# PEER's expert weights: one-hot products into a ring on chip in place of indirect DMAs into a table in DRAM

## The chip, the cores and the metric

The kernel runs on one core of a Trainium2 chip. The metric is the time of one execution on the device in microseconds (us), and the program's own span is what the profile shows. TensorE (PE in the rows) multiplies matrices, VectorE (DVE), ScalarE (ACT) and GpSimd (POOL) do the work on elements, SyncE (SP) issues the loads of the weights. SBUF is the memory on chip, PSUM holds what TensorE sums up, DRAM lies off the chip.

## The reference

One block of a recurrent and attention mixture, with a PEER layer at its end, and after it a second block with four feed-forward parts and two attentions; 256 tokens of 1024 channels, all in fp32. The change is in the PEER layer, which picks 16 of 16384 experts for each of eight heads:

```python
q = (xt @ w_q).reshape(BLOCK, PEER_HEADS, PEER_QDIM)
s1 = jnp.einsum('chd,nd->chn', q[..., :half], keys1).astype(jnp.float32)
s2 = jnp.einsum('chd,nd->chn', q[..., half:], keys2).astype(jnp.float32)
t1, i1 = lax.top_k(s1, PEER_TOPK)
t2, i2 = lax.top_k(s2, PEER_TOPK)
cand = (t1[..., :, None] + t2[..., None, :]).reshape(BLOCK, PEER_HEADS, PEER_TOPK * PEER_TOPK)
ts, sel = lax.top_k(cand, PEER_TOPK)
idx = jnp.take_along_axis(cidx, sel, axis=-1)
g = jax.nn.softmax(ts, axis=-1)
act = jax.nn.gelu(jnp.einsum('chkd,cd->chk', u[idx], xt))
coef = (g * act.astype(jnp.float32)).astype(xt.dtype)
return jnp.einsum('chk,chkd->cd', coef, v[idx])
```

An expert's number is 128 times a key of the first half plus a key of the second, so a token's weights g are a table of 128 x 128 with at most 128 cells that are not zero.

## The kernel before, in words

The kernel does not gather experts. It multiplies all 16384 rows of u with all 256 tokens, takes the gelu, multiplies it by the table of weights G, which is zero at experts that were not chosen, and multiplies that by all rows of v. Weights come in chunks of 128 x 1024 in an order that the list `plan` fixes: a DMA on SP's queue (L117) brings a chunk into one of five `raw` places, ScalarE rounds it to float32r (`whi`, L107), VectorE subtracts that from the raw chunk (`wlo`, L125, in `losplits`), and TensorE multiplies three times (hi by hi, hi by lo, lo by hi; L153 to L155 for a column block, L165 to L169 for a row block). `pump` issues these up to three chunks ahead. Every engine works in the order of the program text.

The PEER part (`peer`, L744) has this order. For each of the eight heads, `query` multiplies two chunks of query weights and scores the two halves against the keys (L779); then QB = 7 blocks of u follow (`ublock`, with the gelu at L860, kept for two blocks in one of RING = 49 tiles of `acts`). Between the blocks `topk_step` lets VectorE do some steps of the pending `unit`s: the first number of steps is BURST times PACE a block, later PACE = 1.75. A unit is one head: four top-16 searches of 128 scores and two of 256 sums (L784 to L789, L804), the softmax (L811, L812, L830 to L832), the chosen keys by one-hot products of 16 x 16 (L824 to L827) and the addresses (L835, L837). At its end it issues 32 indirect DMAs on POOL, 16 for each half of the tokens, one weight per partition each, that add to G in DRAM, with a memset of one element (`spacer`, L841) ahead of each:

```python
for j in range(16):
    nc.gpsimd.memset(spacer, 0.0)
    x = nc.gpsimd.indirect_dma_start(
        out=G, out_offset=bass.IndirectOffsetOnAxis(ap=ad[:, tb, j:j + 1], axis=0),
        in_=gg[:, tb, j:j + 1], in_offset=None, compute_op=OP.add)
```

`gg` has three buffers, so a head's softmax waits for the DMAs of an earlier head. G was set to zero during block 1 by 64 stores of 256 KB on SP's queue (`zero_g`, L742). After 98 blocks of u, POOL loads G in pieces of four blocks (`gload`, L899), VectorE multiplies the gelu by it (L912), `coef` splits the result (`chi`, `clo`, L182, L183), and the rows of v follow, 128 chunks, with the last 30 blocks of u one by one between the first 30 rows. Then come the residual with block 1's final norm, and block 2, which uses the same places for weights and two more of hi and lo each.

Of the kernel before, what the change touches and what calls it, by code (L numbers as in the profile page):

```python
# [8 lines left out]
F32 = mybir.dt.float32  # L9
F32R = mybir.dt.float32r  # L10
# [7 lines left out]
KB = 8  # L18
# [9 lines left out]
RING = 49  # L28
PACE = 1.75
QB = 7  # L30
BURST = 1.4
NBURST = 16
GB = 4
# [12 lines left out]
for _n, _w in (("ident", 128), ("ones", 128), ("iota16", 16), ("tok", 2), ("half", 2)):  # L46
    CST[_n] = (_off, _w)
    _off += _w
# [16 lines left out]

class Net:
    def __init__(self, ctx, tc, A):
        self.tc, self.nc, self.A = tc, tc.nc, A
        self.base = ctx.enter_context(tc.tile_pool(name="base", bufs=1))
        self.raws = ctx.enter_context(tc.tile_pool(name="raws", bufs=5))  # L70
        self.his = ctx.enter_context(tc.tile_pool(name="his", bufs=4))
        self.los = ctx.enter_context(tc.tile_pool(name="los", bufs=4))
# [3 lines left out]
        self.RA, self.SA, self.bufs, self.lim = 5, 3, 4, None  # L76
        self.pools = [(self.his, self.los)]
        self.b2 = 1 << 30
        self.side = []
# [3 lines left out]
        self.ones = self.c("ones")  # L83

# [9 lines left out]
    def pump(self, i, ahead=None):  # L94
        """loads, hi parts (ahead of chunk i) and, one chunk behind them, lo parts"""
        nc = self.nc
        ahead = self.SA if ahead is None else ahead
        self.prefetch(i)
        lim = len(self.plan) if self.lim is None else self.lim
        self.losplits(max(i, self.si - 1))  # L100
        while self.si < min(i + ahead + 1, lim, self.di):
            j = self.si
            self.losplits(j - 1)
            hp, lp = self.pools[0 if j < self.b2 or (j - self.b2) % 6 < 4 else 1]
            self.hi[j] = hp.tile([128, 1024], F32R, name="whi")
            self.lo[j] = lp.tile([128, 1024], F32R, name="wlo")
            nc.scalar.activation(self.hi[j], self.raw[j], AF.Copy)  # L107
            self.si += 1
            if j <= i:
                self.losplits(j)  # L110

    def prefetch(self, i):
        nc = self.nc
        while self.di < min(i + self.RA, len(self.plan)):
            j = self.di
            self.raw[j] = self.raws.tile([128, 1024], F32, name="raw")
            nc.sync.dma_start(out=self.raw[j], in_=self.plan[j])  # L117
            self.di += 1
            if self.side and j >= 10:
                self.side.pop(0)()  # L120

    def losplits(self, n):
        while self.li <= n and self.li < self.si:
            j = self.li
            self.nc.vector.tensor_sub(out=self.lo[j], in0=self.raw.pop(j), in1=self.hi[j].bitcast(F32))  # L125
# [8 lines left out]
    def chunks(self, n):  # L134
        """n chunks that are in use together"""
        i = self.ci
        self.pump(i, self.bufs - 1)
# [19 lines left out]
    def row_a(self, acc, w, xT, k, first, last):  # L157
        """acc[tb*2+half][tokens, 512] += x[tokens, row block k] w[row block k, 1024 columns]."""
# [19 lines left out]
    def split(self, hi, lo, src, scale=None):  # L178
        """hi + lo = src (times a per-partition scale)."""
# [8 lines left out]
    def tail(self, acc, rows):  # L188
        """the last row blocks, one accumulator after the other; rows: (w, xT, k)"""
# [10 lines left out]
    def rstd(self, r, a, b, p=128):  # L200
        """r = (a + b + eps) ** -0.5, one column"""
# [50 lines left out]
    def to_T(self, outs, x, dg, by_k=False):  # L252
        """channel-major halves of gain * (x * r); outs: (xT, gain), with all but the first left to be called"""
# [1201 lines left out]
```

## Time and profile before

| | |
|---|---|
| median of three runs | 2266.77 us (2264.26 to 2267.86) |
| span of the profiled execution | 2265.6 us (no other time of it is given) |
| TensorE busy | 2027.9 us, 90% |
| VectorE busy | 1292.5 us, 57% |
| ScalarE busy | 1065.4 us, 47% |
| GpSimd busy | 559.0 us, 25% |
| read from and written to DRAM | 367.58 MB and 17.96 MB |

How to read it: busy times are sums over the whole program, and the stages have different limits, so a share says little by itself. TensorE's busy time counts instructions in flight. A row of a group gives busy time in us and the mean length of one instruction in ns; consecutive instructions of one engine overlap a little, so their sum exceeds the time they fill. "Idle before" names what the engine waited for. PEclk is the clock that TensorE was granted, 1.00 being 2.4 GHz and 0.50 being 1.2 GHz.

### The profile page before, as it was taken

How to read it: one execution, taken by the hardware profiler on the slowest of the kernel's cores; microseconds unless marked ns; L12 is line 12 of the kernel's file. 1: busy time of each engine (PE TensorE's matmuls, PEld its weight loads, DVE VectorE, ACT ScalarE, POOL GpSimd, SP SyncE). 2: the span in 40 equal slices, each digit the busy share in tenths (PEclk: the TensorE clock that was granted, in tenths of full speed). 3: DMA queues.
4: the chain of work that ended last, by engine and by line, in shares of the span. 5: the costliest groups of instructions: out<-in, count | busy, mean ns of one | idle time of the engine just before them, and what ended most of it. 6: DMA issues, size and time to landing. Idle time of an engine off the chain costs nothing.

```text
span 2265.6 us, 35450 instructions
## 1 busy us (share of the span) xinstructions
PE 2027.9 (90%) x13868; PEld 1843.6 (81%) x13868; DVE 1292.5 (57%) x2242; ACT 1065.4 (47%) x1623; POOL 559.0 (25%) x687
## 2 busy tenths in 40 slices
PE   8999999975655029999999999999999999999998
PEld 8977999975655029988888899987999999988998
DVE  6565789855542015556666655559654654576444
ACT  5565565532332014444444544467544544466443
POOL 1211138888888850000000100002000000010000
PEclk9999999997878559999999999999999999999999
DMA  7755857755555236666776555542555455534553
GB/s 243 236 156 152 276 146 178 196 122 103 112 121 113 0 65 212 207 214 232 242 235 236 193 193 187 180 164 97 174 187 195 159 188 193 188 111 141 194 194 113
DMA packets 150455, 387.85 MB, mean 171 GB/s; under 512 B 49408, under 2 KB 51968, under 8 KB 150288
## 3 DMA queue, kind: packets, MB, share of 16 engines
q1 hardware_dynamic: 107520, 366.30, 48.8%
q0 software_dynamic: 41616, 17.58, 6.7%
q8 instruction: 108, 1.77, 0.3%
q10 hardware_dynamic: 1152, 1.71, 0.3%
q14 instruction: 59, 0.48, 0.1%
HBM read 367.58 MB, written 17.96 MB: 170 GB/s over the span
## 4 chain that ended last, share of the span: by engine, by line
PE 59%; POOL 10%; DVE 4%; issue 2%; ACT 1%; DMA 0%; POOLq 0%; DVEq 0%; ACTq 0%
PE b L153 10%; PE b L155 9%; PE b L154 9%; PE acc L165 9%; PE acc L167 9%; POOL coef L842 9%; PE acc L169 9%; DVE wlo L125 2%; PE acc L196 1%; PE acc L198 1%; PE acc L197 1%; PE acc L260 0%; DMA coef<-gg,ad 0%; PE b L1231 0%; PE b L1079 0%
## 5 line engine op out<-in xcount | busy, mean ns | idle before, releaser
L125 DVE TENSOR_TENSOR wlo<-raw,whi 128x1024 fp32r<-128x1024 f32 x660 | 784.6, 1225 | 97.2 <-ACT whi L107 89.7
L107 ACT ACTIVATE whi<-raw 128x1024 fp32r<-128x1024 f32 x660 | 678.0, 1052 | 208.5 <-issue 83.0
L155 PE MATMUL b<-xhi,wlo 128*128 128x256 f32 x2416 | 678.8, 281 | 84.0 <-DVE wlo L125 84.0
L153 PE MATMUL b<-xhi,whi 128*128 128x256 f32 x2416 | 680.3, 282 | 0.4 <-DVE lb L1081 0.4
L154 PE MATMUL b<-xlo,whi 128*128 128x256 f32 x2416 | 677.2, 280 | 0.0
L155 PEld LDWEIGHTS b<-xhi,wlo 128*128 128x128 f32 x2416 | 462.7, 192 | 86.1 <-DVE wlo L125 86.0
L153 PEld LDWEIGHTS b<-xhi,whi 128*128 128x128 f32 x2416 | 457.5, 189 | 5.1 <-DVE lb L1081 0.6
L154 PEld LDWEIGHTS b<-xlo,whi 128*128 128x128 f32 x2416 | 457.1, 189 | 3.8
L842 POOL DMA_INDIRECT coef<-gg,ad x256 | 431.1, 1684 | 93.5 <-issue 92.4
L165 PE MATMUL acc<-whi,chi 128*128 128x512 f32 x500 | 158.0, 397 | 122.8 <-ACT chi L182 122.8
L203 POOL TENSOR_SCALAR r<-ss 128x1 f32<-128x1 f32 x16 | 4.7, 297 | 856.6 <-ACT acc L230 487.9
L165 PEld LDWEIGHTS acc<-whi,chi 128*128 128x128 f32 x500 | 92.1, 189 | 143.3 <-ACT chi L182 123.0
L1002 DVE TENSOR_TENSOR silu<-silu,b 128x256 f32<-128x256 f32 x88 | 37.1, 421 | 294.0 <-PE b L155 287.7
L841 POOL MEMSET spacer<- 1x1 f32 x256 | 160.2, 626 | 0.0
L169 PE MATMUL acc<-whi,clo 128*128 128x512 f32 x500 | 157.9, 397 | 0.0
L167 PE MATMUL acc<-wlo,chi 128*128 128x512 f32 x500 | 157.9, 397 | 0.0
L182 ACT ACTIVATE fhi<-silu 128x256 fp32r<-128x256 f32 x88 | 36.8, 418 | 241.4 <-DVE silu L1002 241.4
L183 DVE TENSOR_TENSOR clo<-act,chi 128x512 fp32r<-128x512 f32 x64 | 44.2, 691 | 155.1 <-ACT chi L182 155.1
L182 ACT ACTIVATE chi<-act 128x512 fp32r<-128x512 f32 x64 | 40.3, 630 | 182.5 <-DVE act L912 122.9
L899 POOL DMA_DIRECT2D gt<-coef x32 | 24.1, 754 | 395.0 <-DVE act L912 393.0
L912 DVE TENSOR_TENSOR act<-act,gt 128x512 f32<-128x512 f32 x64 | 43.9, 686 | 124.0 <-DMA gt<-coef 124.0
L155 PE MATMUL b<-ohi,wlo 128*128 128x256 f32 x400 | 113.2, 283 | 1.5 <-DVE wlo L125 1.5
(384 smaller groups left out, 3307.3 us busy)
## 6 DMA issues: line engine op xcount, KB each, us to landing
raw<-ffn_in SPq DMA_DIRECT2D x176, 512.0 KB
raw<-peer_u SPq DMA_DIRECT2D x128, 512.0 KB
raw<-peer_v SPq DMA_DIRECT2D x128, 512.0 KB
raw<-ffn_out SPq DMA_DIRECT2D x88, 512.0 KB
raw<-w_in SPq DMA_DIRECT2D x38, 512.0 KB
coef<-zeros SPq DMA_DIRECT2D x64, 256.0 KB
gt<-coef POOLq DMA_DIRECT2D x32, 512.0 KB
raw<-peer_wq SPq DMA_DIRECT2D x16, 512.0 KB
```

Source lines behind the costliest of these rows:

```text
L107: nc.scalar.activation(self.hi[j], self.raw[j], AF.Copy)
L125: self.nc.vector.tensor_sub(out=self.lo[j], in0=self.raw.pop(j), in1=self.hi[j].bitcast(F32))
L153: mm(ps, whi[:, s], xhi[:, k, n0:n1], start=(k == 0), stop=False)
L154: mm(ps, whi[:, s], xlo[:, k, n0:n1], start=False, stop=False)
L155: mm(ps, wlo[:, s], xhi[:, k, n0:n1], start=False, stop=(k == nk - 1))
L165: mm(acc[tb * 2 + h], xhi[:, k, t], whi[:, h * 512:(h + 1) * 512], start=first, stop=False)
L167: mm(acc[tb * 2 + h], xhi[:, k, t], wlo[:, h * 512:(h + 1) * 512], start=False, stop=False)
L169: mm(acc[tb * 2 + h], xlo[:, k, t], whi[:, h * 512:(h + 1) * 512], start=False, stop=last)
L182: nc.scalar.activation(hi, src, AF.Copy)
L183: nc.vector.tensor_sub(out=lo, in0=src, in1=hi.bitcast(F32))
L841: nc.gpsimd.memset(spacer, 0.0)
L842: x = nc.gpsimd.indirect_dma_start(out=G, out_offset=bass.IndirectOffsetOnAxis(ap=ad[:, tb, j:j + 1], axis=0), in_=gg[:, tb, j:j + 1], in_ ...
```

## The change

The table of weights is no longer added up in DRAM. The top-k units only note, for each token, head and choice, the two keys and the score (`res`). After the units one softmax over all heads follows, and TensorE transposes the two key tables and the weights so that the 128 pairs of head and choice lie on partitions (`rT`, kept in the second half of h). For one token, `e` is the one-hot matrix of the second keys (128 pairs x 128 keys, made by POOL) and `a` that of the first keys, scaled by the weights (made by VectorE); one fp32 product gives the token's whole 128 x 128 table. Four tokens make a group: their product is multiplied into the gelus that already lie in `ring` (VectorE) and copied to the blocks whose gelu is still to come (ScalarE). `ring` holds the gelus or weights of all 128 blocks, 128 KB in each partition. 64 groups run between 26 blocks of u.

Around this: QB is 6 and PACE 1.7; 66 blocks of u (NU1) are in the head part, two more cover the transposes, 26 are in the loop (NU2 = 28 with those two), 34 between rows of v. The chosen keys' multiplication moves from VectorE to POOL. The weights' places become lists of free slots (`Slots`): two raw places are fixed, three lie in block 1's memory, later in rows of the ring that are not in use, in h (which is saved to DRAM and brought back twelve chunks before the end of v), and in block 2's memory; at most six loads are ahead. Keys are loaded on POOL's queue behind the save of h. The stores of zeros are gone.

```diff
-RING = 49
-PACE = 1.75
-QB = 7
+NU1 = 66
+NU2 = 28
+PACE = 1.7
+QB = 6
...
-        self.RA, self.SA, self.bufs, self.lim = 5, 3, 4, None
+        self.rs, self.hs, self.ls = Slots(), Slots(), Slots()
+        self.places(self.base, 2, 4, 4)
+        self.RA, self.SA, self.done = 6, 3, 0
...
-    def zero_g(self, pool):
...
-            self.side.append(lambda a=a: nc.sync.dma_start(out=gv[a], in_=z))
...
+            ring = one.tile([128, EXP_BLOCKS, S], F32, name="ring")
...
+            nc.gpsimd.dma_start(out=hd_, in_=h_)
+            back = self.b2 - 12
+            self.rs.add(h[:, 0, :], back)
+            for b in (100, 104, 108):
+                self.rs.add(ring[:, b:b + 4, :].rearrange("p a b -> p (a b)"), self.p1 + 16 + NU1)
+            keys = carve((2, 128))
+            nc.gpsimd.dma_start(out=keys[:, 0, :], in_=A["keys1"])
+            nc.gpsimd.dma_start(out=keys[:, 1, :], in_=A["keys2"])
...
                     for j in range(2):
-                        oh = tk.tile([128, 16, 16], F32, name="oh")
...
-                        nc.vector.tensor_mul(out=oh, in0=oh, in1=i12f[:, tb, j, None, :].to_broadcast([128, 16, 16]))
-                        nc.vector.tensor_reduce(out=ex[:, tb, j, :], in_=oh, axis=AX.X, op=OP.add)
...
-                for tb in tbs:
-                    for j in range(16):
-                        nc.gpsimd.memset(spacer, 0.0)
-                        x = nc.gpsimd.indirect_dma_start(
...
+                        nc.gpsimd.tensor_mul(out=oh[:, tb, j], in0=oh[:, tb, j],
+                                             in1=i12f[:, tb, j, None, :].to_broadcast([128, 16, 16]))
+                    late.append(lambda tb=tb: nc.vector.tensor_reduce(out=res[:, 0:2, tb, hk], in_=oh[:, tb], axis=AX.X,
+                                                                      op=OP.add))
...
+                p = self.bank(S)
+                self.lin_b(p, self.chunk(), 0, x2T, KB, 0, S)
+                if n:
+                    nc.scalar.activation(p[:, :n], p[:, :n], AF.Gelu_apprx_tanh)
+                if n < S:
+                    nc.scalar.activation(ring[:, b, n:], p[:, n:], AF.Gelu_apprx_tanh)
+                if n:
+                    nc.vector.tensor_mul(out=ring[:, b, :n], in0=p[:, :n], in1=ring[:, b, :n])
...
-            gload(0)
-            gload(1)
...
+            def onehots(g):
+                if g >= NG:
+                    return
+                t0 = 4 * g
+                e, a = et[g % 3], at[g % 2]
+                for i in range(4):
+                    nc.gpsimd.tensor_scalar(e[:, i, :], iota, rT[:, 1, t0 + i:t0 + i + 1], None, op0=OP.is_equal)
+                for i in range(4):
+                    nc.vector.tensor_scalar(a[:, i, :], iota, rT[:, 0, t0 + i:t0 + i + 1], rT[:, 2, t0 + i:t0 + i + 1],
+                                            op0=OP.is_equal, op1=OP.mult)
+                st[g] = (e, a)
...
+                for i in range(4):
+                    mm(p[:, i * 128:(i + 1) * 128], e[:, i, :], a[:, i, :], start=True, stop=True)
+                pg = p.rearrange("p (t b) -> p b t", b=128)
+                onehots(g + 1)
+                nc.vector.tensor_mul(out=ring[:, :nb, t0:t0 + 4], in0=pg[:, :nb, :], in1=ring[:, :nb, t0:t0 + 4])
+                nc.scalar.activation(ring[:, nb:, t0:t0 + 4], pg[:, nb:, :], AF.Copy)
+                built[0] = g + 1
+
+            onehots(0)
+            g = 0
+            for i in range(2, NU2):
+                ublock(u)
+                u += 1
+                while g * (NU2 - 2) < NG * (i - 1):
+                    group(g, u)
+                    g += 1
...
-                c = act.pop(b2)
-                nc.vector.tensor_mul(out=c, in0=c, in1=gt[b // GB][:, b % GB:b % GB + 2, :].rearrange("p a b -> p (a b)"))
```

On POOL the order before, from the end of block 1 through the PEER part, was this (the two rows that follow each other 256 times stand once):

```order
L203 TENSOR_SCALAR r<-ss 128x1
L204 TENSOR_TENSOR r<-r,cst 128x1
L841 MEMSET spacer 1x1
L842 DMA coef<-gg,ad 4194304x1
...
L842 DMA coef<-gg,ad 4194304x1
L899 DMA gt<-coef 128x4x256 x32
```

and it is now this, from the same place (`work` holds the one-hot matrices, `coef` is the DRAM table, which now only keeps h):

```order
L242 TENSOR_SCALAR r<-ss 128x1
L243 TENSOR_TENSOR r<-r,cst 128x1
L804 DMA coef<-h 128x2048
L810 DMA ring<-keys 128x128
L811 DMA ring<-keys 128x128
L877 TENSOR_TENSOR work<-work,ring 128x256 x32
L968 TENSOR_SCALAR work<-cst,h 128x128 x256
L1020 DMA ring<-final_g 128x512 x2
L1026 DMA h<-coef 128x2048
```

The 256 DMAs and their spacers went, 32 products and 256 one-hots came, and the save of h stands ahead of the keys.

On VectorE, at the end of the last unit and the begin of the v part, the order before was:

```order
L837 SCALAR_TENSOR_TENSOR ad<-ex 128x16
L125 TENSOR_TENSOR wlo<-raw,whi 128x1024 x22
L912 TENSOR_TENSOR act<-act,gt 128x512
L183 TENSOR_TENSOR clo<-act,chi 128x512
L912 TENSOR_TENSOR act<-act,gt 128x512
L183 TENSOR_TENSOR clo<-act,chi 128x512
L125 TENSOR_TENSOR wlo<-raw,whi 128x1024 x4
```

and in the second and third turn of the new loop it is:

```order
L163 TENSOR_TENSOR wlo_70<-raw_61,whi_66 128x1024
L905 TENSOR_TENSOR ring<-b,ring 128x12
L970 TENSOR_SCALAR work<-cst,h 128x128 x4
L983 TENSOR_TENSOR ring<-acc,ring 128x70x4
L970 TENSOR_SCALAR work<-cst,h 128x128 x4
L983 TENSOR_TENSOR ring<-acc,ring 128x70x4
L163 TENSOR_TENSOR wlo_67<-raw_62,whi_63 128x1024
L905 TENSOR_TENSOR ring<-b,ring 128x20
L970 TENSOR_SCALAR work<-cst,h 128x128 x4
L983 TENSOR_TENSOR ring<-acc,ring 128x71x4
```

A turn has one subtraction (L163), the product with the gelu of its own block (L905, waiting for ScalarE), and for each group four one-hots of the next group (L970) ahead of the product into the ring (L983, waiting for TensorE).

## Rows read from the trace of the kernel before

**Rows 1.** Busy time by stretches: PE, PEld, DVE, ACT, POOL, then PEclk, DMA share, GB/s

```profile
299.00:327.40 28.40, 26.95 (x227) 26.13 (x227) 24.98 (x81) 17.26 (x22) 8.16 (x9) 1.00 0.52 156
...
405.60:431.50 25.90, 25.65 (x226) 25.46 (x226) 24.78 (x68) 14.85 (x18) 22.73 (x24) 1.00 0.76 187
550.00:600.00 50.00, 21.00 (x166) 20.80 (x165) 19.76 (x54) 12.76 (x15) 43.38 (x50) 0.69 0.43 73
700.00:750.00 50.00, 11.86 (x105) 11.66 (x103) 4.18 (x4) 5.82 (x7) 43.14 (x54) 0.64 0.37 51
750.00:800.00 50.00, 0.00 (x0) 0.00 (x0) 0.00 (x0) 0.00 (x0) 42.86 (x55) 0.50 0.22 0
```

**Rows 2.** Waits from 280 to 840 us: who waited for whom, total, times, longest

```profile
DVE act L912 <- DMA gt<-coef: 124.0, 1, 124.0
...
DVE gg L811 <- DMA coef<-gg,ad: 94.4, 4, 31.5
...
PE b L155 <- DVE wlo L125: 84.0, 9, 29.0
```

**Rows 3.** Costliest groups, POOL's: busy, mean ns of one, idle time before

```profile
L842 POOL DMA_INDIRECT coef<-gg,ad x256 | 431.1, 1684 | 93.5 <-issue 92.4 <-DVE wlo L125 0.5 <-DVE ex L827 0.3
L841 POOL MEMSET spacer<- 1x1 f32 x256 | 160.2, 626 | 0.0
```

**Rows 4.** ScalarE in order of time, one head: start, us, instruction, idle before

```profile
379.71 0.39 ACT L772 ACTIVATE q<-b 128x256 f32<-128x256 f32 x1 [1.77 <-PE b L155]
...
397.45 0.60 ACT L860 ACTIVATE act<-b 128x512 f32<-128x512 f32 x1 [1.77 <-PE b L155]
402.89 0.60 ACT L860 ACTIVATE act<-b 128x512 f32<-128x512 f32 x1 [1.77 <-PE b L155]
405.62 0.39 ACT L772 ACTIVATE q<-b 128x256 f32<-128x256 f32 x1 [1.17 <-PE b L155]
```

**Rows 5.** TensorE in order of time: PEER's begin and the first row of v

```profile
292.94 1.50 PE L260 MATMUL acc<-dg,h 128*128 128x128 f32 x12
294.20 0.37 PE L153 MATMUL b<-xhi,whi 128*128 128x256 f32 x1
...
834.67 1.22 PE L165 MATMUL acc<-whi,chi 128*128 128x512 f32 x2 [122.81 <-ACT chi L182]
```

**Rows 6.** VectorE's groups by shape: busy, mean ns of one, idle before

```profile
L125 DVE TENSOR_TENSOR wlo<-raw,whi 128x1024 fp32r<-128x1024 f32 x69 | 83.0, 1217 | 9.9 <-ACT whi L107 8.1 <-issue 1.8
L826 DVE TENSOR_TENSOR oh<-oh,i12f 128x256 f32<-128x256 f32 x22 | 9.5, 434 | 0.8
...
L912 DVE TENSOR_TENSOR act<-act,gt 128x512 f32<-128x512 f32 x64 | 43.9, 686 | 124.0 <-DMA gt<-coef 124.0
```

**Rows 7.** VectorE and POOL in order of time, in block 1

```profile
45.85 0.99 DVE L405 TENSOR_SCALAR cd<-cst,cs 128x128 f32<-128x128 f32 x5
46.77 0.40 DVE L483 TENSOR_SCALAR y<-xrp,pv 128x272 f32<-128x272 f32 x1
...
67.91 0.84 POOL L467 TENSOR_TENSOR iy<-iy,y 128x272 f32<-128x272 f32 x1 [2.71 <-ACT iy L466]
68.03 0.88 DVE L483 TENSOR_SCALAR y<-xrp,pv 128x272 f32<-128x272 f32 x1
```

**Rows 8.** POOL's scalings: one line's least, median, most ns; and a group

```profile
L948 POOL TENSOR_SCALAR h<-act,r x4: 683/693/1401, 1284.7 to 1288.0; 128x512 f32<-128x512 f32 x4
...
L203 POOL TENSOR_SCALAR r<-ss 128x1 f32<-128x1 f32 x16 | 4.7, 297 | 856.6 <-ACT acc L230 487.9 <-ACT acc L1325 187.5 <-issue 179.0
```

**Rows 9.** ScalarE in order of time, gelus beside the first rows of v

```profile
848.66 0.60 ACT L860 ACTIVATE act<-b 128x512 f32<-128x512 f32 x1 [1.78 <-PE b L155]
...
859.86 0.60 ACT L860 ACTIVATE act<-b 128x512 f32<-128x512 f32 x1 [1.72 <-PE b L155]
...
871.11 0.60 ACT L860 ACTIVATE act<-b 128x512 f32<-128x512 f32 x1 [1.72 <-PE b L155]
```

**Rows 10.** Busy time in a stretch of block 1, columns as in rows 1

```profile
224.00:232.00 8.00, 6.50 (x52) 6.16 (x52) 6.22 (x10) 7.90 (x16) 4.02 (x4) 1.00 0.07 13
```

More of the change, by code (lines that the diff above doesn't have):

```diff
@@ L63, with __init__, add, take @@
 NC2 = _off
+class Slots:
+    def __init__(self):
+        self.all, self.occ, self.clock = [], {}, 0
+    def add(self, ap, until=1 << 30):
+        self.all.append([ap, until, self.clock])
+    def take(self, j):
+        free = [s for s in self.all if j < s[1] and not any(o is s for o in self.occ.values())]
+        if not free:
+            return None
+        s = min(free, key=lambda s: (s[1], s[2]))
+        self.occ[j] = s
+        return s[0]
+    def free(self, j):
+        self.clock += 1
+        self.occ.pop(j)[2] = self.clock
 class Net:
@@ L83, in __init__, with places @@
         self.ones = self.c("ones")
+    def places(self, pool, nr, nh, nl, until=1 << 30):
+        for n, k, sl in (("raw", nr, self.rs), ("whi", nh, self.hs), ("wlo", nl, self.ls)):
+            for i in range(k):
+                dt = F32 if n == "raw" else F32R
+                sl.add(pool.tile([128, 1024], dt, name=f"{n}{i}", bufs=1), until)
     def c(self, n):
@@ L97, in pump @@
         ahead = self.SA if ahead is None else ahead
+        while self.done < min(i, self.ci):
+            self.hs.free(self.done)
+            self.ls.free(self.done)
+            self.done += 1
         self.prefetch(i)
-        lim = len(self.plan) if self.lim is None else self.lim
         self.losplits(max(i, self.si - 1))
-        while self.si < min(i + ahead + 1, lim, self.di):
+        while self.si < min(i + ahead + 1, self.di):
             j = self.si
             self.losplits(j - 1)
[L104 to L107, printed above, removed]
+            t = self.hs.take(j)
+            if t is None:
+                assert j > i
+                break
+            self.hi[j] = t
+            nc.scalar.activation(t, self.raw[j], AF.Copy)
             self.si += 1
@@ L115, in prefetch @@
             j = self.di
-            self.raw[j] = self.raws.tile([128, 1024], F32, name="raw")
-            nc.sync.dma_start(out=self.raw[j], in_=self.plan[j])
+            t = self.rs.take(j)
+            if t is None:
+                break
+            self.raw[j] = t
+            nc.sync.dma_start(out=t, in_=self.plan[j])
             self.di += 1
-            if self.side and j >= 10:
-                self.side.pop(0)()
     def losplits(self, n):
@@ L300, in block1 @@
             sm = ctx.enter_context(tc.tile_pool(name="b1sm", bufs=2))
+            self.places(one, 3, 0, 0, self.p1)
             def T8(name, dt=F32, n=T):
@@ new lines, in peer @@
+            for c0, n in ((0, 2), (2, 1)):
+                p = self.ps.tile([128, 512], F32, name="acc", tag="acc")
+                for i in range(2 * n):
+                    nc.tensor.transpose(p[:, i * 128:(i + 1) * 128], res[:, c0 + i // 2, i % 2, :], self.ident)
+                nc.scalar.activation(rT[:, c0:c0 + n, :].rearrange("p a b -> p (a b)"), p[:, :n * S], AF.Copy)
+            used[1] = 0
+            et = [carve((4, 128), F32, 1) for _ in range(3)]
+            at = [carve((4, 128), F32, 1) for _ in range(2)]
@@ L935, in peer @@
             self.tail(acc, rows)
-            hg = [acts.tile([128, 512], F32, name="act") for _ in range(4)]
+            hg = [room(20 + 2 * i, 2) for i in range(4)]
             dg, r = self.residual(spool, h, acc, 1.0, (hg, gain), ahead=True)
```

219 lines of the change are left out of this document (110 added, 109 removed).

## The prediction

> **What bounds the kernel now.** I read the busy time by stretches first, then the waits of the PEER part, then the group of POOL's indirect DMAs, then single instructions for their pace. The stretches show where TensorE stops: in the head loop it is busy for 25.65 of 25.90 us, in three later stretches of 50 us for 21.00, 11.86 and 0 us, while POOL is busy for 43 of 50 in all three [rows 1]. The waits name the cause: once, for 124.0 us, VectorE waits for the load of the table of coefficients, and four times, 94.4 us together, it waits at a head's softmax (L811) for an indirect DMA. Behind that wait on VectorE's queue stand the subtractions that make wlo, so TensorE waits 84.0 us for wlo [rows 2]. POOL is the source: 256 indirect DMAs of 1.684 us and as many spacers of 0.626 us, 591 us of POOL's own time [rows 3], where the stretch on TensorE's path takes 834.67 - 294.20 = 540.5 us from the first query matmul to the first row of v [rows 5].
>
> What TensorE itself needs there follows from its pace. Two u blocks take 402.89 - 397.45 = 5.44 us, 2.72 us for one chunk; a head of nine chunks takes 405.62 - 379.71 = 25.91 us, so 1.43 us are left for its four key products [rows 4]. 114 chunks and 8 heads are 321.5 us: 219 us of the 540.5 are waiting.
>
> **The change, part by part.** All POOL work of the stretch, the 124.0 us and the 94.4 us go. In their place, on TensorE's path from 294.20 on:
>
> 1. Sixteen query chunks and 66 u blocks, 82 x 2.72 = 223.0 us, and 8 x 1.43 = 11.4 us of key products.
>
> 2. Stalls of that part. VectorE must keep up. Before, a head had 24.78 us of it [rows 1]; nine subtractions of 1.217 us [rows 6] are 11.0, so 13.8 us are top-k, 15.75 of a unit's 21 steps: 18.4 us a unit. Now four multiplications of 0.434 us [rows 6] go to POOL and the addresses go, some 2.3 us; 16.1 us a unit, of which 13.6 of 17 steps fall on a head, 12.9 us, with eight subtractions 22.6 us against TensorE's 8 x 2.72 + 1.43 = 23.2 us. The cover is 0.6 us a head: thin. I take 5.5 us: 1.45 us as the first head loses now (26.95 busy of 28.40 [rows 1]), the rest for POOL's products and for the keys, which now follow the 1 MB save of h on POOL's queue. The ends are 0 and 22 (32 products of 0.84 us on POOL [rows 7] that all hold VectorE up, less 8 x 0.6).
>
> 3. Two u blocks, 5.4 us, and six transposes at 0.21 us (twelve passes of fp32 128x128 fill 292.94 to 294.20, two to a product [rows 5]), 1.3 us. Scores, softmax and the first one-hot group lie beside these and block 68.
>
> 4. The loop: 26 u blocks with 64 groups of four tokens, 2.46 groups to a block. TensorE: 2.72 + 2.46 x 4 x 0.21 + 0.2 for the changes of type = 5.0 us a turn. VectorE: four one-hots of 128 columns. Five with one scalar of the partition, the last of them shorter, take 0.99 us; with two scalars 272 columns take 0.40 us [rows 7]; I take 0.25 us, 1.0 a group. Then the product of PSUM and ring, 4 x 69 to 94 elements, on average 328: between 0.434 us for 256 and 0.686 us for 512 [rows 6], less some 0.07 us of overlap, 0.43 us. That it steps through the ring in pieces of four no row shows; the pace of whole rows is taken. With one subtraction of 1.2 and 0.3 us for the gelu part: 2.46 x 1.43 + 1.5 = 5.0 us a turn, level with TensorE. POOL: 9.85 one-hots a turn. Between 0.297 us for one column and 0.683 us for 512 [rows 8] a line gives 0.39 us, 3.84 us a turn.
>
> These three don't run freely side by side. A VectorE instruction of 0.40 us took 0.88 us where a POOL product of 0.84 us ran beside it: 0.88 began at 68.03 and ended 0.16 us after POOL did [rows 7]. So a POOL instruction costs VectorE about (0.88 - 0.40)/0.84 = 0.57 of its length, where VectorE reads two operands of SBUF or scales one. Such work is 2.46 x 1.0 + 1.2 = 3.66 of its 5.0 us, 73%. 3.84 x 0.73 x 0.57 = 1.6 us: 6.6 us a turn, 26 x 6.6 = 172 us. The ends: 5.1 us (133 us) without collisions, 8.85 us (230 us) if VectorE's 3.66, POOL's 3.84 and the free 1.35 us come one after the other. I stay at the middle, where the one measured pair lies.
>
> The Trainium skill (SBUF — State Buffer, Who interferes with whom) states it more harshly: VectorE and GpSimd share a pair of ports under an exclusive lock, whoever comes first holds it for the whole instruction, and the other one fully blocks. It speaks against this change; the pair above agrees in kind, but its 0.48 us is less than POOL's 0.84.
>
> 5. The first coefficients wait for the last group's product and their split: 1.5 us, two steps of about 0.69 us [rows 6].
>
> 6. The v part gets four more u blocks beside it, 10.9 us. It runs on TensorE (two rows and two blocks in 871.11 - 859.86 = 11.25 us). Its first pair now takes 848.66 - 834.67 = 14.0 us [rows 5, 9], after 120 us of pause; with the pause those 2.7 us go. The 64 multiplications by the table on VectorE were beside TensorE and give nothing.
>
> 7. At nothing: the 64 stores of zeros (beside block 1's matmuls), h saved and brought back (1 MB each; the load starts eleven rows of v before its use, some 30 us), the new places of the weights (only three raw places in the loop, but a turn there is twice as long as a chunk). If that cover is gone, h back late costs up to 6 us and block 2's first chunks up to 3 us.
>
> Sum: 223.0 + 11.4 + 5.5 + 6.7 + 172 + 1.5 = 420.1 us for 540.5; 120.4 us gained, less 10.9, plus 2.7: 112 us. The profiled execution spans 2265.6 us, and no other time of it is given; the median of the three runs is 1.2 us above. 2265.6 - 112.2 + 1.2 = 2154.6: **2155 us**.
>
> **The rivals.** *No collisions*: POOL runs three groups ahead and meets VectorE only in its PSUM products. The loop is 133 us, the time 2155 - 39 = 2116. For it: POOL has the shorter list; against it: the pair in [rows 7].
>
> *One after the other*: the loop takes 8.85 us a turn, 230 us, and the time is 2213. For it: in [rows 7] neither engine gets on while the other is at it, and 9.85 hand-overs a turn can each cost something; against it: part of VectorE's wait was hidden in its own start. This is the Trainium skill's lock, from the section named above, taken by its word.
>
> *TensorE's clock*: it is granted 0.69 in a stretch where it is busy for 21.00 of 50 us [rows 1], and 1.00 in one where it is busy for 6.50 of 8 [rows 10]. If the loop, busy at 5.0 of 6.6, fell to the lower level of 1.2 GHz, a turn would be 10 us on TensorE, 260 us, the time 2243. Against it: its gaps there are about 1 us each, those of [rows 1] some 30 us.
>
> *Slower than before*: POOL's one-hots become the bound. The gain of 112 us is gone at 284 us for the loop, 10.9 us a turn, 1.11 us for each of the 9.85 one-hots. The longest POOL instruction of this form took 1.401 us, with 512 columns and VectorE beside it [rows 8]; 1.2 us for 128 columns would give 307 us and 2290. For it: no row shows a comparison on POOL. Against it: the same form without VectorE takes 0.683 us for four times the columns.
>
> **How the numbers follow.** My forecast (a turn of 5.7 to 7.3 us) has 0.52, no collisions 0.24, one after the other 0.14, the clock 0.06, slower 0.03, and 0.01 for a loss that just eats the gain. The range takes in the first three: from 2116 less the 5.5 us of stalls, 2110, to 2213. A measurement of this kernel tells some 0.2%, 4.5 us, from no change. Faster 0.96, the same 0.01, slower 0.03.
>
> **What would show it.** Right: no wait for a DMA of coefficients is left; the head loop keeps 2.72 us a chunk; the first row of v starts at about 714 us; in the loop VectorE is the busiest, its four one-hots with POOL beside them take about 1.5 us instead of 1.0, and TensorE waits there for VectorE's one-hots. Wrong: PEclk below 1.0 in the loop (the clock), one-hots on POOL far from 0.39 us, products into the ring far from 0.43 us (the stride), TensorE waiting for POOL rather than VectorE, or wlo late in the head loop (the cover of 0.6 us).

## The result, and the profile after

The changed kernel takes 2177.99 us, median of four runs (2174.22 to 2178.89), against 2265.7 us (2264.26 to 2267.86) of the kernel before: a ratio of 0.961, interval 0.9596 to 0.9623. The forecast was 2155 us with a range of 2110 to 2213. The time lies in the range, 23 us above the forecast. The profiled execution took 2177.61 us, its span is 2175.8 us, 89.8 us shorter than before, where 112.2 were forecast.

The busy time by stretches of the kernel after answers to [rows 1] and shows the loop, 550 to 700 us:

```profile
405.60:431.50 25.90, 25.65 (x220) 25.46 (x219) 21.77 (x62) 12.15 (x15) 3.73 (x4) 1.00 0.52 164
550.00:600.00 50.00, 45.75 (x318) 40.62 (x318) 38.12 (x105) 17.66 (x39) 50.00 (x75) 0.97 0.27 83
600.00:650.00 50.00, 45.05 (x328) 40.29 (x327) 38.36 (x108) 16.97 (x41) 50.00 (x75) 1.00 0.27 85
```

The third number of busy time is VectorE's, the fifth POOL's. In the loop POOL is busy for 50.00 of 50 us and VectorE for 38. VectorE was forecast to be the busiest. The waits from 290 to 730 us, which answer to [rows 2]:

```profile
PEld acc L980 <- POOL work L968: 30.8, 73, 0.7
POOL work L968 <- ACT h L955: 23.1, 1, 23.1
...
PE acc L980 <- DVE work L970: 12.0, 27, 0.6
```

PEld is TensorE's loading of weights. No wait for a DMA of coefficients is left. The products of one-hots (L980) wait first of all for POOL's one-hots (L968), 73 times, and only 27 times for VectorE's (L970). What the two lines take, from the views of the two lines (least, median and most ns, first and last start):

```profile
L968 POOL TENSOR_SCALAR work<-cst,h x256: 596/602/1662, 548.8 to 723.6; 128x128 f32<-128x128 f32 x128
```

```profile
L970 DVE TENSOR_SCALAR work<-cst,h x256: 328/338/481, 549.0 to 723.6; 128x128 f32<-128x128 f32 x128
```

POOL's one-hot takes 0.602 us and not 0.39. The 256 of them fill 175.4 us without a gap (the group's busy time), 0.685 us from start to start on average, and that is the loop.

The average hides two kinds, and the 1662 in the row of L968 points at the second. In each of the 26 turns one of POOL's one-hots runs beside VectorE's subtraction of two tensors, which makes wlo:

```profile
604.33 1.21 DVE L163 TENSOR_TENSOR wlo<-raw,whi 128x1024 fp32r<-128x1024 f32 x1
```

```profile
604.48 1.53 POOL L968 TENSOR_SCALAR work<-cst,h 128x128 f32<-128x128 f32 x1
```

By the timelines of the two engines, all 26 of these take 1.33 to 1.66 us and end 0.40 to 0.48 us after the subtraction; the next one-hot starts 1.52 us after such a one, and 0.59 us after any other. So about 26 x (1.52 - 0.59) = 24 of the 175.4 us are POOL held up by VectorE's subtraction. The subtraction itself keeps its 1.21 us. An estimate from these two figures: without the hold the 256 one-hots would fill 256 x 0.59 = 151 us. What the loop meets then is seen below, in e12_pair.

Where the 89.8 us come from follows from the beginnings of the stages; TensorE's and ScalarE's single instructions of the kernel after (in this order block 1's residual sum, the first PEER matmul, the first row of v, PEER's residual sum, and the first silu, block 2's first activation):

```profile
287.50 0.60 ACT L269 ACTIVATE acc<-h 128x512 f32<-128x512 f32 x1 [1.89 <-DVE h L266]
...
297.57 0.37 PE L192 MATMUL b<-xhi,whi 128*128 128x256 f32 x1
...
726.17 1.22 PE L204 MATMUL acc<-whi,chi 128*128 128x512 f32 x2 [1.48 <-ACT chi L221]
...
1176.17 0.60 ACT L269 ACTIVATE acc<-h 128x512 f32<-128x512 f32 x1 [1.89 <-DVE h L266]
...
1200.59 0.38 ACT L1100 ACTIVATE silu<-b 128x256 f32<-128x256 f32 x1
```

and those of the kernel before, beside [rows 5]:

```profile
284.18 0.60 ACT L230 ACTIVATE acc<-h 128x512 f32<-128x512 f32 x1 [1.89 <-DVE h L227]
...
1275.15 0.60 ACT L230 ACTIVATE acc<-h 128x512 f32<-128x512 f32 x1 [1.89 <-DVE h L227]
...
1292.93 0.38 ACT L1001 ACTIVATE silu<-b 128x256 f32<-128x256 f32 x1
```

| stage | before | after | forecast |
|---|---|---|---|
| to block 1's residual sum | 284.18 | 287.50 (+3.3) | no change |
| first PEER matmul to POOL's first one-hot (548.8) | | 251.2 | 246.6 |
| from there to the first row of v | | 177.4 | 173.5 |
| both together | 540.5 | 428.6 (-111.9) | 420.1 |
| first row of v to PEER's residual sum | 440.5 | 450.0 (+9.5) | +8.2 |
| block 2, from there to the end | 990.5 | 999.6 (+9.2) | no change |

### The profile page after: what moved, and what is told of

Same layout as the page of the kernel before. It is cut to its first block, busy times and chain, and to the rows that moved or that the text cites. A ratio compares the mean times of both kernels' runs of the same rounds, so it can differ in the third digit from the quotient of the medians.

```text
span 2175.8 us, 36723 instructions
## 1 busy us (share of the span) xinstructions
PE 2122.0 (98%) x14386; PEld 1914.6 (88%) x14386; DVE 1349.3 (62%) x2458; ACT 1078.1 (50%) x1720; POOL 309.7 (14%) x436
## 3 DMA queue, kind: packets, MB, share of 16 engines
q8 instruction: 114, 1.87, 0.3%
## 4 chain that ended last, share of the span: by engine, by line
PE 82%; POOL 9%; DVE 5%; issue 2%; ACT 2%; DMA 0%; SPq 0%; POOLq 0%; DVEq 0%; ACTq 0%
PE b L192 15%; PE b L194 15%; PE b L193 15%; PE acc L204 10%; PE acc L206 10%; PE acc L208 10%; POOL work L968 8%; DVE wlo L163 2%; PE acc L235 1%; PE acc L237 1%; PE acc L236 1%; PE acc L299 1%; PE acc L676 0%; PE acc L677 0%; PE b L505 0%
## 5 line engine op out<-in xcount | busy, mean ns | idle before, releaser
L163 DVE TENSOR_TENSOR wlo<-raw,whi 128x1024 fp32r<-128x1024 f32 x451 | 537.4, 1227 | 44.9 <-ACT whi L138 43.2
L138 ACT ACTIVATE whi<-raw 128x1024 fp32r<-128x1024 f32 x451 | 463.8, 1052 | 73.0 <-PE acc L208 43.6
L968 POOL TENSOR_SCALAR work<-cst,h 128x128 f32<-128x128 f32 x256 | 175.4, 706 | 23.1 <-ACT h L955 23.1
L138 ACT ACTIVATE whi<-ring 128x1024 fp32r<-128x1024 f32 x106 | 112.0, 1058 | 114.6 <-issue 43.3
L163 DVE TENSOR_TENSOR wlo<-ring,whi 128x1024 fp32r<-128x1024 f32 x106 | 132.0, 1246 | 12.9 <-ACT whi L138 12.8
L163 DVE TENSOR_TENSOR wlo<-h,whi 128x1024 fp32r<-128x1024 f32 x103 | 126.9, 1232 | 7.6 <-ACT whi L138 7.6
L222 DVE TENSOR_TENSOR clo<-ring,chi 128x512 fp32r<-128x512 f32 x64 | 44.2, 693 | 120.8 <-ACT chi L221 118.9
L206 PEld LDWEIGHTS acc<-wlo,chi 128*128 128x128 f32 x500 | 94.3, 189 | 22.8
L208 PEld LDWEIGHTS acc<-whi,clo 128*128 128x128 f32 x500 | 94.2, 188 | 22.8
L192 PE MATMUL b<-ohi,whi 128*128 128x256 f32 x400 | 112.4, 281 | 0.0
```

The costliest lines, as they stand in the source:

```text
L138: nc.scalar.activation(t, self.raw[j], AF.Copy)
L163: self.nc.vector.tensor_sub(out=t, in0=self.raw.pop(j), in1=self.hi[j].bitcast(F32))
L192: mm(ps, whi[:, s], xhi[:, k, n0:n1], start=(k == 0), stop=False)
L206: mm(acc[tb * 2 + h], xhi[:, k, t], wlo[:, h * 512:(h + 1) * 512], start=False, stop=False)
L208: mm(acc[tb * 2 + h], xlo[:, k, t], whi[:, h * 512:(h + 1) * 512], start=False, stop=last)
L222: nc.vector.tensor_sub(out=lo, in0=src, in1=hi.bitcast(F32))
```

## The experiments

All start from the changed kernel unless they name another. Each ratio is to the kernel before, run on the same chip, with its 95% interval; differences in us to the change are of medians from different chips, so the ratios decide. Two theories stand from the first reading. A: POOL's one-hot simply costs 0.60 us, about 0.69 from start to start, and POOL sets the loop. B: it costs 0.39 us, as forecast, and the rest is waiting for VectorE. C, that TensorE sets the loop, goes along.

**e3_alone.** VectorE's one-hots are left out from the third group on.

```diff
-                for i in range(4):
+                for i in range(4 if g < 2 else 0):
                     nc.vector.tensor_scalar(a[:, i, :], iota, rT[:, 0, t0 + i:t0 + i + 1], rT[:, 2, t0 + i:t0 + i + 1],
                                             op0=OP.is_equal, op1=OP.mult)
```

> Leaves out VectorE's one-hots of expert halves times gate from the third group of four tokens on (the coefficients are wrong after that), so POOL's 256 one-hots run beside a VectorE that has 1.2 us less to do in each of the 64 groups. Theory A (a POOL one-hot costs 0.60 us by itself and about 0.69 from start to start, whatever VectorE does): POOL stays full in the loop, L968 keeps its median of 602 ns, the loop stays at 170 to 178 us and the time within 5 us of 2178. Theory B (it costs about 0.39 us and the rest is waiting for VectorE's accesses): L968 falls to 400 to 500 ns, the loop to what TensorE needs, 26 u blocks x 2.8 + 64 products x 1.05 = 140 us, and the time to about 2145. Theory C (TensorE sets the loop): the time stays, but POOL shows idle time in the loop.

Ratio 0.9593 (0.9574 to 0.9612), 2172.65 us: no difference from the change that can be told. The stretch and POOL's line:

```profile
600.00:650.00 50.00, 47.32 (x332) 40.54 (x331) 20.61 (x35) 17.66 (x42) 50.00 (x74) 1.00 0.25 84
```

```profile
L968 POOL TENSOR_SCALAR work<-cst,h x256: 596/603/1672, 547.8 to 720.7; 128x128 f32<-128x128 f32 x128
```

VectorE falls from 38 to 21 of 50 us, POOL stays at 50 and its one-hot at 0.603 us. A stands for the 0.60 us and for POOL setting the loop, and B falls; C falls too, since POOL has no gap. The step from 0.60 to 0.685 is not A's, though: the subtractions stay in this run, and 26 one-hots of 1.49 to 1.67 us are still there.

**e2_split.** One of POOL's four goes to VectorE.

```diff
-                    nc.gpsimd.tensor_scalar(e[:, i, :], iota, rT[:, 1, t0 + i:t0 + i + 1], None, op0=OP.is_equal)
+                    eng = nc.vector if i == 3 else nc.gpsimd
+                    eng.tensor_scalar(e[:, i, :], iota, rT[:, 1, t0 + i:t0 + i + 1], None, op0=OP.is_equal)
```

> One of POOL's four one-hots in each group goes to VectorE. Theory A: POOL needs 3 x 0.69 = 2.07 us a group in place of 2.76, VectorE 2.2 + 0.3 = 2.5 and becomes the bound, 64 x 2.5 = 160 in place of 177: 15 to 20 us faster, about 2160. Theory B (the two engines exclude each other): what the two need together falls by only 0.1 us a group, 6 us or less: 2172 to 2178. Theory C: no change.

Ratio 0.9567 (0.9551 to 0.9583), 2166.89 us, 11 us less than the change: more than B's 6 and less than A's 15. POOL now stands idle for 44.9 us, waiting for TensorE to free one of the three buffers, and yet TensorE waits 38.2 us for POOL's one-hots and 13.0 for VectorE's. From POOL's first one-hot to the first row of v it is 169.1 us in place of 177.4, 8 us less and not 17; e12_pair shows why.

**e1_wide.** Two POOL instructions of 512 columns in place of four of 128.

```diff
-                for i in range(4):
-                    nc.gpsimd.tensor_scalar(e[:, i, :], iota, rT[:, 1, t0 + i:t0 + i + 1], None, op0=OP.is_equal)
+                nc.gpsimd.tensor_sub(out=e, in0=iota[:, None, :].to_broadcast([128, 4, 128]),
+                                     in1=rT[:, 1, t0:t0 + 4, None].to_broadcast([128, 4, 128]))
+                nc.gpsimd.tensor_scalar(e, e, 0.0, None, op0=OP.is_equal)
```

> POOL makes the four one-hots of a group with two instructions of 128x512 (number minus index for four tokens, then equal to zero) instead of four of 128x128. Theory A with a price that is mostly for the instruction: 1.2 to 1.4 for the subtraction and 0.7 for the comparison, about 2.0 us a group; TensorE (140 us for the loop) and VectorE (2.2 us a group) become the bound: 20 to 30 us faster, about 2153. Theory A with a price that goes by elements: 4 x 0.6 + 4 x 0.7 = 5.2 us a group, 64 x 2.4 more: about 2330. Theory B: more accesses to wait for, slower, 2190 or more. Theory C: no change.

Ratio 0.9701 (0.9679 to 0.9724), 2197.73 us, 20 us slower than the change. Neither price of A was right: the comparison of 512 columns takes 1.49 us, so a column costs (1.490 - 0.602)/384 = 2.3 ns and the instruction itself some 0.3. POOL needs 2.57 us for a group that nothing holds up; with 21 instructions of 2.13 to 2.44 us beside VectorE's subtraction it is busy for (75.6 + 107.8)/64 = 2.87 us a group, where the change has 4 x 0.685 = 2.74. And a new wait appears, in POOL's and VectorE's instructions one by one:

```profile
601.27 1.03 POOL L967 TENSOR_TENSOR work<-cst,h 128x512 f32<-128x512 f32 x1
602.39 1.49 POOL L969 TENSOR_SCALAR work<-work 128x512 f32<-128x512 f32 x1
```

```profile
601.31 1.07 DVE L971 TENSOR_SCALAR work<-cst,h 128x128 f32<-128x128 f32 x1
602.30 0.77 DVE L971 TENSOR_SCALAR work<-cst,h 128x128 f32<-128x128 f32 x1
603.00 0.33 DVE L971 TENSOR_SCALAR work<-cst,h 128x128 f32<-128x128 f32 x1
```

VectorE's one-hot, begun 0.04 us after POOL's subtraction, lasts 1.07 us and ends with it; free of it, it takes 0.33.

**e4_nu2.** Six more blocks of u by the end of the loop.

```diff
-NU2 = 28
+NU2 = 34
```

> 34 blocks of u in place of 28 are computed by the end of the loop (NU2 = 34), so six leave the part of the rows of v. Theory A (and B): POOL paces the loop, 64 x 2.76 = 177 us, in which TensorE has 6 x 2.8 = 17 us to spare; the loop stays at 177 to 182 and the v part shortens by 6 x 2.8: 12 to 17 us faster, about 2163. Theory C: the loop grows by what the v part loses, no change within 4 us.

Ratio 0.9549 (0.9528 to 0.9571), 2162.92 us, 15 us less than the change. The six blocks of u fit under POOL's time: its one-hots run from 549.1 to 730.5, 181.3 us in place of 175.4, and the v part lost 18 us. C falls here too.

```profile
L968 POOL TENSOR_SCALAR work<-cst,h x256: 594/602/1664, 549.1 to 729.9; 128x128 f32<-128x128 f32 x128
```

The 256 one-hots are the same, and so is their median; but six more blocks bring six more subtractions, and by the timeline 32 one-hots in place of 26 are held up. At 0.93 us each that is 5.6 of the 6.0 us by which POOL's time grew.

**e8_price.** What does the 0.60 us pay for? POOL multiplies in place of comparing.

```diff
-                    nc.gpsimd.tensor_scalar(e[:, i, :], iota, rT[:, 1, t0 + i:t0 + i + 1], None, op0=OP.is_equal)
+                    nc.gpsimd.tensor_scalar(e[:, i, :], iota, rT[:, 1, t0 + i:t0 + i + 1], None, op0=OP.mult)
```

> POOL's 256 comparisons become 256 multiplications by the same scalars, of the same size (the coefficients are wrong after that). Theory A1 (the price goes with the operation: on POOL a comparison takes 0.30 us and 2.3 ns a column, which the 0.60 us of 128 columns and the 1.49 us of 512 give, a multiplication 0.30 us and 0.75 ns a column): L968 falls to about 0.39 us, POOL needs under 2 us a group and idles, the loop goes to what VectorE and TensorE leave, 150 to 168 us, and the time to 2150 to 2168. Theory A2 (the price is that of the form, whatever the operation): L968 stays at 0.60, the time at 2174 to 2180.

Ratio 0.9608 (0.9592 to 0.9624), 2176.5 us; A2. The multiplication costs the same:

```profile
L968 POOL TENSOR_SCALAR work<-cst,h x256: 593/599/1662, 548.7 to 723.8; 128x128 f32<-128x128 f32 x128
```

**e9_twoop.** The row that had given 0.39, POOL's scaling of 512 columns in 0.683 us [rows 8], has two operations. So the comparison gets a second one, times 1.0.

```diff
-                    nc.gpsimd.tensor_scalar(e[:, i, :], iota, rT[:, 1, t0 + i:t0 + i + 1], None, op0=OP.is_equal)
+                    nc.gpsimd.tensor_scalar(e[:, i, :], iota, rT[:, 1, t0 + i:t0 + i + 1], 1.0, op0=OP.is_equal,
+                                            op1=OP.mult)
```

> POOL's comparison gets a second operation, times 1.0, as the scalings of POOL in the residual have (0.683 us for 128x512 with two operations, against 1.49 us for 128x512 with one in the run with two wide instructions). Theory F (on POOL the form with one operation is the slow one, whatever the operation): L968 falls to about 0.39 us, POOL needs under 2 us of a group and idles, the loop goes from 177 to 150 to 168 us, and the time to 2150 to 2168. Rival G (the 0.60 us has another cause: the second operand, or the tiles' place): L968 stays at 0.60 or grows, the time at 2174 or more.

Ratio 0.9723 (0.9707 to 0.9739), 2202.11 us. F falls: the second operation costs 0.11 us more.

```profile
L968 POOL TENSOR_SCALAR work<-cst,h x256: 707/713/1772, 547.1 to 748.7; 128x128 f32<-128x128 f32 x128
```

**e12_pair.** What is left of that row is its pair of multiplications.

```diff
-                    nc.gpsimd.tensor_scalar(e[:, i, :], iota, rT[:, 1, t0 + i:t0 + i + 1], None, op0=OP.is_equal)
+                    nc.gpsimd.tensor_scalar(e[:, i, :], iota, rT[:, 1, t0 + i:t0 + i + 1], 1.0, op0=OP.mult,
+                                            op1=OP.mult)
```

> POOL's 256 comparisons become a pair of multiplications, by the same scalar and by 1.0, the form of the scalings in the residual (128x512 in 0.683 us), at 128 columns (the coefficients are wrong after that). Theory H (POOL has a quick path for this pair of operations, and the estimate of 0.39 us was right for it and wrong for a comparison): L968 at 0.35 to 0.45 us, POOL idles in the loop, 2150 to 2168. Rival I (the pair costs what comparison and multiplication cost, 0.71 us; the scalings in the residual are quick for a reason of their own): L968 at 0.65 to 0.75 us and the time near 2200.

Ratio 0.9547 (0.9528 to 0.9566), 2162.56 us. H stands:

```profile
L968 POOL TENSOR_SCALAR work<-cst,h x256: 368/375/1412, 547.8 to 702.6; 128x128 f32<-128x128 f32 x128
```

```profile
600.00:650.00 50.00, 45.74 (x350) 42.82 (x349) 42.81 (x116) 18.02 (x44) 29.56 (x80) 1.00 0.28 85
```

This run is the loop as it was forecast, with one-hots of 0.375 us on POOL. It takes 162 us from POOL's first one-hot to the last product, POOL idles, and the first row of v starts 711.13 - 296.51 = 414.6 us after the first PEER matmul (forecast: 420.1). It also shows the next bound: between two blocks of u two or three groups follow one another, and in such a run each takes 1.29 to 1.41 us (in the middle of the loop 2 groups in 2.58 us, 3 in 4.22), where its eight passes alone take 1.05. TensorE waits there, 19.4 us for POOL's one-hots and 8.8 for VectorE's, while POOL waits 57.2 us for a free buffer: the one-hots are only one or two groups ahead when such a run begins. More buffers, for which no memory is left, were not tried.

**e6_act34.** A way around POOL's price that keeps the computation, on top of e4_nu2: one of four comparisons on ScalarE.

```diff
-                for i in range(4):
+                for i in range(3):
                     nc.gpsimd.tensor_scalar(e[:, i, :], iota, rT[:, 1, t0 + i:t0 + i + 1], None, op0=OP.is_equal)
+                nc.scalar.activation(e[:, 3, :], iota, AF.Square, bias=rT[:, 1, t0 + 3:t0 + 4], scale=-1.0)
+                nc.scalar.activation(e[:, 3, :], e[:, 3, :], AF.Relu, bias=self.ones[:, 0:1], scale=-1.0)
```

> One of POOL's four comparisons goes to ScalarE, as the square of the difference and then 1 minus it, cut at zero; and 34 blocks of u in place of 28 by the end of the loop. Theory A: POOL needs 3 x 0.69 x 64 = 132 us, TensorE 32 x 2.8 + 64 x 1.05 = 157, VectorE about 155; the loop takes 157 to 168 in place of the 182 with 34 blocks alone, 2140 to 2150. Rival (ScalarE, which has the gelus, the copies of the ring's rest and the hi parts before it, delivers the one-hot late): the loop stays over 175 and the time at 2157 or more.

Ratio 0.954 (0.9524 to 0.9556), 2160.47 us: in the rival's range, and not to be told from e4_nu2 by the times. The loop is 175 us (546.9 to 722) where 157 to 168 were expected; ScalarE's two pieces take 0.39 and 0.40 us and the trace shows no wait for them, so the rival's time came and its cause did not. From 550 to 710 us TensorE waits 19.6 us for POOL's one-hots and 13.5 for VectorE's, as in e12_pair in the runs of groups, and POOL 48.6 us for a buffer.

**e5_raws and e10_raws2.** Block 2's first chunks wait for a place. Both kernels give the base pool a third raw place. e5_raws takes its memory by moving the third buffer of POOL's one-hots into the ring's last blocks; e10_raws2 does without that buffer.

```diff
-        self.places(self.base, 2, 4, 4)
+        self.places(self.base, 3, 4, 4)
...
-            et = [carve((4, 128), F32, 1) for _ in range(3)]
+            et = [carve((4, 128), F32, 1) for _ in range(2)]
```

These two edits stand in both kernels, and so does a smaller `work`; e5_raws also has `et.append(sct[0]...)`, the third buffer in its new place, and e10_raws2 takes the two buffers in turn.

> A third place for raw weights in the base pool (its 4 KB come from the third buffer of POOL's one-hots, which moves into memory of the scores, idle by then). Theory P (block 2 starts late because only two of its chunks have a place before the last readers of the blocks of gelu are done): a third chunk of block 2 lies loaded at the residual sum, ScalarE's waits for raw<-ffn_in shrink by about 2.5 to 5 us, the first silu comes 18 to 21 us after the residual sum in place of 24.4, and the time falls by 3 to 6 us to about 2173. Rival (the chunks are late for another reason: POOL's scalings or ScalarE's order): the first silu stays 24 us behind and the time within 1.5 us.

> The third place for raw weights again, now with two buffers of POOL's one-hots in place of three, and none in the ring. The loop is paced by POOL and should grow by 0 to 8 us from the missing buffer. Theory P (block 2 waits for a place): the first silu 20 to 22 us behind the residual sum in place of 24.4. If the loop holds at 177, the time falls by 3 to 5 us.

e5_raws: ratio 0.9706 (0.969 to 0.9722), 2197.43 us. The choice of memory was a mistake of mine: ScalarE copies each group's product into all blocks to the ring's end, so it writes over that buffer (the coefficients are wrong after that), and copy and one-hots wait for each other (ScalarE 34.0 us for POOL); POOL's one-hots now end at 744. The start of block 2 still got shorter, 21.6 us from residual sum to silu.

e10_raws2: ratio 0.9597 (0.9581 to 0.9613), 2174.1 us, too near the change for the times to tell. The trace tells: 1197.06 - 1175.59 = 21.5 us to the first silu in place of 24.4, and ScalarE's waits for the loads went from the first of these rows (change) to the second (e10_raws2):

```profile
ACT whi L138 <- DMA raw<-ffn_in: 4.9, 2, 2.5
```

```profile
ACT whi L138 <- DMA raw<-ffn_in: 2.1, 1, 2.1
```

P stands, for about 3 of the 6.6 us that block 2's start lost: the ten kernels with two places take 23.0 to 25.2 us here, the three with a third place 20.9 to 21.6. Places for more chunks were not tried. The loop did not miss the buffer (548.3 to 722.9).

**e7_block1.** Block 1 prepares 3 chunks ahead where several are taken at once.

```diff
-        self.pump(i, 5)
+        self.pump(i, 3 if i < self.p1 else 5)
```

> In block 1 a call for several chunks prepares 3 chunks ahead, as before the change, and not 5, so that VectorE has one wlo in place of two ahead of the last softmax scaling. Theory S (that second wlo makes TensorE wait 1.9 us for the scaling, after which its clock falls to the lower level for some us): the wait is back at 0.5 us, no stretch of 5 us between 215 and 230 has a clock below 0.9, the residual sum of block 1 is back at 284 to 285 and the time 2 to 4 us lower. Rival (block 1 is slower for another reason, the zeros' transfers that went or the places): it stays at 286 to 288.

Ratio 0.9604 (0.9588 to 0.962), 2174.71 us; again the trace tells, first the change, then e7_block1:

```profile
215.00:220.00 5.00, 3.13 (x25) 2.75 (x25) 4.91 (x8) 1.74 (x5) 2.46 (x2) 1.00 0.33 89
220.00:225.00 5.00, 5.00 (x21) 3.29 (x20) 0.43 (x2) 0.49 (x1) 0.00 (x0) 0.59 0.66 229
225.00:230.00 5.00, 5.00 (x24) 3.35 (x23) 0.79 (x2) 1.19 (x2) 0.00 (x0) 0.73 0.00 0
```

```profile
215.00:220.00 5.00, 4.53 (x30) 3.01 (x29) 3.43 (x7) 1.67 (x3) 2.37 (x2) 1.00 0.45 141
220.00:225.00 5.00, 5.00 (x33) 3.81 (x34) 0.76 (x2) 1.16 (x2) 0.00 (x0) 1.00 0.18 72
```

In the change VectorE has two wlo, 3.23 us, ahead of the last softmax scaling; TensorE waits 1.87 us for it, and its granted clock in the next two stretches is 0.59 and 0.73, near the lower level of 1.2 GHz for part of them. With one wlo the wait is 0.47 us, the clock stays at 1.00, and the residual sum comes at 284.27. S stands for the order of the two wlo and for this pair of runs. The link from the wait to the clock is not shown as a rule: all eleven kernels without this edit have the wait of 1.87 us, in nine the clock of 220 to 225 us is 0.52 to 0.70, and in e6_act34 and e9_twoop it is 1.00; there the residual sum comes at 285.72 and 285.98 (elsewhere without the edit at 286.14 to 288.19). e6_act34:

```profile
220.00:225.00 5.00, 4.27 (x27) 2.96 (x28) 1.64 (x6) 0.49 (x1) 0.00 (x0) 1.00 0.82 283
```

From the begin of the wait to the residual sum it is 69.9 us in the change, 67.2 with the edit and 66.9 in e6_act34. So it is the lower clock that costs, some 3 us here, and not the wait, since a later wait of 1.49 us takes its place in e7_block1; why the clock falls in one run and not in another stays open.

**e11_best.** e6_act34 with the edits of e7_block1 and e10_raws2.

> The parts that helped, together: one comparison of four on ScalarE and 34 blocks of u by the end of the loop (2160.5 alone), the preparation of 3 chunks in block 1 (3.3 us less alone), the third place for raw weights with two buffers of POOL's one-hots (3.9 us less alone). If the parts add up: 2153, ratio to the kernel before 0.951. Rival: with two buffers POOL can no longer run ahead of TensorE while a block of u is computed, which cost nothing while POOL was behind anyway; the loop then grows by up to 8 us over the 175 of the run with ScalarE's share, and the time stays at 2157 to 2162.

Ratio 0.9518 (0.9502 to 0.9534), 2156.09 us, the fastest kernel of this study that computes everything, 22 us under the change. It stays 3 us above the sum of the parts, and not for the reason of the rival: the first row of v starts at 723.69 as in e6_act34 (723.79). Block 1's sum stands at 285.72 in both: in e6_act34 the clock had not fallen, so that edit had nothing to give there. The start of block 2 takes 20.9 us.

## Why the prediction was right, and where it was not

- **The whole.** All POOL work on DMAs and its waits went, and 111.9 us of the stretch with them; 120.4 were forecast. Right in kind, 8.5 us off.
- **Step 1, the pace of the head part.** 2.72 us a chunk was 2.80: gelus of two blocks now come every 5.60 us, where [rows 4] have 5.44.

```profile
497.21 0.60 ACT L895 ACTIVATE ring<-b 128x512 f32<-128x512 f32 x1 [1.85 <-PE b L194]
502.81 0.60 ACT L895 ACTIVATE ring<-b 128x512 f32<-128x512 f32 x1 [1.85 <-PE b L194]
```

  That is 41 x 0.16 = 6.6 us. All twelve kernels of the experiments have this 5.60. Why TensorE starts its matmuls every 0.1167 us in place of 0.1133, with the clock granted at 1.00 in both, stays open. In the kernel before itself the blocks of u beside the first rows of v, from 860 us on, have 0.118, so 2.72 was the pace of one stretch.
- **Step 2, the stalls.** The part took 251.2 - 246.6 = 4.6 us more than forecast, less than the pace alone; so the 5.5 us of stalls were set a little high (TensorE stands idle for 251.2 - 246.9 = 4.3 us there). The thin cover held: TensorE is busy for 25.65 of 25.90 us.
- **Step 4, the loop.** 172 us were forecast, 175.4 came, and the agreement is an accident: one term was too small, another too large and on the wrong engine, and the two errors cancelled out. "Between 0.297 us for one column and 0.683 us for 512 a line gives 0.39 us" was the mis-sized term. The line was drawn between additions and multiplications in pairs and used for a comparison, whose columns cost 2.3 ns; at 0.59 us from start to start, POOL's 9.85 one-hots a turn need 5.8 us in place of 3.84, more than the 5.0 forecast for VectorE and TensorE. The collision term, 1.6 us a turn, was the second. It was read from a POOL product of two tensors [rows 7], which holds VectorE up, and charged to VectorE beside POOL's one-hots; but there VectorE's keep a median of 338 ns against 328 at least. The collision that came is the other way round: VectorE's subtraction holds up one POOL one-hot a turn, 0.93 us. 5.8 + 0.93 is the 6.75 us of a turn (175.4/26). A row of the prediction had this collision, the 1.401 us of [rows 8]: that scaling began 0.37 us after a subtraction and outlasted it.

```profile
1284.32 1.22 DVE L125 TENSOR_TENSOR wlo<-raw,whi 128x1024 fp32r<-128x1024 f32 x1
```

```profile
1284.69 1.40 POOL L948 TENSOR_SCALAR h<-act,r 128x512 f32<-128x512 f32 x1
```

  So "VectorE is the busiest" was wrong, and "TensorE waiting for POOL" was the sign, named beforehand, that showed it.
- **VectorE's and TensorE's share of step 4.** VectorE's four one-hots take 1.15 to 1.3 us in place of 1.0, the product into the ring 0.435 to 0.55 where 0.43 stood, so the stride costs little. "5.0 us a turn" without collisions was too low: e12_pair, with POOL idle, needs 162/26 = 6.2. Groups come in runs of two and three, and a mean over the turn hides that the one-hots are never far enough ahead for a run.
- **Step 6.** +9.5 us against +8.2.
- **Step 7, "at nothing".** Here most of the miss lies, 12.5 of 22.4 us. Block 2's first chunks were given up to 3 us; they lost 6.6, and the rest of the 9.2 came after the first silu and was not taken apart. Block 1 lost 3.3 us, behind an order of two wlo that I had not looked for and the lower clock that followed in this run. The zero stores that went gave nothing, as forecast.
- **The rivals.** One after the other, the Trainium skill's lock (SBUF — State Buffer, Who interferes with whom): the Trainium skill speaks there of VectorE instructions with two inputs in SBUF or in a mode that uses two ports. Where VectorE subtracts two tensors, the trace agrees, POOL's one-hot 1.53 us for 0.60; where VectorE scaled beside POOL's subtraction of two tensors, e1_wide agrees, 1.07 us for 0.33; where VectorE's one-hots run beside POOL's, nothing is held up, 338 ns, and no row shows in which mode they run. No collisions: true of VectorE's one-hots and false of POOL's beside the subtraction, and even e12_pair gets to 2162 and not to 2116. The clock: 0.97 to 1.00 in the loop, so no. POOL as the bound: it became the bound, at 0.685 us on average and not at the 1.11 from which it would have eaten the gain; e9_twoop shows how the way there begins, 0.79 us and 2202.

## What to carry to other kernels

A price by elements holds for one engine, one operation and one number of operations; before a line is drawn between two rows, look whether they do the same thing. When a sum comes out right, compare the wait that ends last with the one the sum rests on: here the time agreed, and the engine did not. Beside a median look at the longest instruction of a group and at what ran beside it: the hold on 26 of 256 one-hots made up 24 us. Edits costed at nothing need the order of the neighbouring engine around each place where several chunks are taken at once.

## What the runs showed of the hardware that I had not expected

- On POOL a tensor_scalar of 128 columns costs 0.602 us as a comparison and 0.599 as one multiplication, 0.713 as a comparison and a multiplication, and 0.375 as two multiplications. With 512 columns it is 1.49 us as a comparison (with a constant in place of a column of scalars), and 0.683 as two multiplications [rows 8]. Which other pairs are quick was not tried.
- VectorE's one-hots are held up by POOL's operation on two tensors until it ends (1.07 us for 0.33 in e1_wide), and by POOL's one-hots hardly at all (338 ns against 328). VectorE's subtraction of two tensors holds up the POOL one-hot beside it, 1.53 us for 0.60, in all 26 turns of the change and all 32 of e4_nu2, and keeps its own 1.21 us.
- A wait of TensorE of 1.87 us was followed by a granted clock of 0.59 and 0.73; one of 0.47 us at the same place was not, but neither was the same 1.87 us in e6_act34 and e9_twoop.
